# A dilated 3x3 convolution on one core: every load of x and every store cut into slices of 16 partitions

## The chip, the cores and the metric

The kernel runs on one core of a Trainium2 chip. The metric is the device time of one execution in microseconds. Each kernel was run several times; runs over 1.5% above the fastest of the same kernel are called slow, and the ratios below use fast runs alone. The program uses no other core of the chip.

## The reference

A convolution of 16 images (64 channels in, 128 out, 64x64 pixels, 3x3 taps, dilation 2, padding 2), all in float32.

```python
batch, c_in, h, w, c_out, k, dilation = 16, 64, 64, 64, 128, 3, 2
x_pad = np.pad(x, ((0, 0), (0, 0), (pad, pad), (pad, pad)), mode='constant')     # pad = 2
for kh in range(k):
    for kw in range(k):
        output[b, co] += weight[co, ci, kh, kw] * x_pad[b, ci, kh*dilation:kh*dilation+h, kw*dilation:kw*dilation+w]
```

x is 16.8 MB and the output 33.6 MB. With the weights the core must move about 50.6 MB.

## The kernel before

Two images at a time fill the 128 partitions (2 x 64 channels). One channel of one image is one DRAM row of 64 x 64 float32, 16 KB, and fills one SBUF partition. ACT casts x to float16, DVE adds row pairs, PE multiplies (it computes pairs of output rows with fewer products than the plain sum), ACT and DVE evacuate PSUM into a float32 output tile, and SP issues all loads and stores.

The parts that the change touches:

```python
x32pool = ctx.enter_context(tc.tile_pool(name="x32pool", bufs=3))
opool = ctx.enter_context(tc.tile_pool(name="opool", bufs=3))
# ... cut ...
def load(pb, rows):
    t = x32pool.tile([P, HW], f32, tag="x32", name="x32")
    x32_tiles[pb] = t
    lo = 0
    for hi in rows:
        nc.sync.dma_start(out=t[:, lo * W : hi * W], in_=x_pair[pb, :, lo * W : hi * W])
        lo = hi
# ... cut ...
def store(pb, m, lo, hi):
    nc.sync.dma_start(
        out=out_img[2 * pb + m, :, lo * W : hi * W],
        in_=o_tiles[pb][:, m * HW + lo * W : m * HW + hi * W],
    )
# ... cut ...
first = [[hi for _, hi in chunk_rows], [32 + d, H], [H]]   # pair 0 in four loads, pair 1 in two
for pb in range(min(3, npairs)):
    load(pb, first[pb])
# ... cut: the main loop over 32 groups of 16 image rows; at the end of a group ...
    if ahead[0] >= NG * (freed[0] + 1) and freed[0] + 3 < npairs:
        load(freed[0] + 3, [H])
        freed[0] += 1
    if pb == 0 and g % 2 == 1:
        for m in range(2):
            store(pb, m, (g - 1) * GR, (g + 1) * GR)
    elif pb > 0 and g == NG - 1:
        for m in range(2):
            store(pb, m, 0, H)
```

## Time and profile before

| what | value | where it is read |
|---|---|---|
| time | 129.94 us, median of 3 runs | runs |
| span of the profiled run | 126.5 us | page |
| PE busy | 83% | page, part 1 |
| DMA queue | 50.63 MB, 96.3% of 16 engines' span | page, part 3 |
| 16384-byte packets | 611 ns, at the 10th, 50th and 90th percentile | DMA packet records of the trace, 60 to 110 us |

These are lines of the page of the kernel before: the span in 40 equal slices (the busy share of the 16 DMA engines in tenths, and what they moved), then the queue, then two kinds of DMA issues (how many, the size of each, the median time from issue to landing).

```profile
DMA  4999999999999999999999999999999999989990
GB/s 134 319 410 405 456 420 409 386 425 427 438 443 404 300 420 414 432 425 445 425 414 435 427 435 425 425 430 425 435 425 430 435 425 430 425 383 425 425 430 26
q1 hardware_dynamic: 4464, 50.63, 96.3%
...
out_dram<-osb SPq DMA_DIRECT2D x14, 2048.0 KB, 15.6
```

The DMA engines are busy nearly everywhere at about 425 GB/s. The next line is a stretch of time from the windows view: start and end, length, busy us (and instructions) of PE, PE weight loads, DVE, ACT and POOL, then the granted clock, the DMA share and GB/s.

```profile
60.00:110.00 50.00, 50.00 (x488) 23.65 (x486) 42.94 (x47) 28.88 (x30) 0.00 (x0) 1.00 1.01 429
```

PE is busy throughout as well, but the timeline shows which of the two ends last: the last evacuation is over at 112.7 us, the last two stores are issued then, and the span ends at 126.5 us with transfers alone.

```profile
111.52 1.22 DVE L220 TENSOR_TENSOR osb<-psB,p_sb 128x1024 f32<-128x1024 f32 x1
112.76 0.81 SPq L100 DMA_DIRECT2D out_dram<-osb  x2
```

So the 50.63 MB set the time: at 429 GB/s they take 118 us of the 126.5. A packet of 16384 bytes in 611 ns is 26.8 GB/s, and 16 engines at that rate are 429 GB/s. That fits the Trainium skill, "DMA: Bandwidth & Descriptors", section "The descriptor swizzle": in a transfer of 128 partitions each engine writes one SBUF port of its own.

### The profile page before, as it was taken

The numbers are of one execution on the slowest core, as the hardware profiler recorded it, in microseconds if no ns is written. First come the engines' busy times: TensorE is split into PE (matmuls) and PEld (weight loads), VectorE is DVE, ScalarE is ACT, GpSimd is POOL, SyncE is SP. The second block draws the span as 40 slices with busy tenths as digits, with TensorE's granted clock in tenths as the row PEclk, the third lists the DMA queues.
The fourth block names the chain that finished last, engine by engine and source line by source line (L and its number), as shares of the span: only waits on it lengthen the run. The fifth ranks groups of instructions, "written<-read, shape, count | busy, mean of one in ns | idle before, by whom it ended". The sixth has DMA issues, their size and how long they took to land.

```text
span 126.5 us, 2316 instructions
## 1 busy us (share of the span) xinstructions
PE 105.4 (83%) x989; PEld 48.7 (39%) x989; DVE 89.9 (71%) x105; ACT 66.8 (53%) x71; POOL 0.7 (1%) x6
## 2 busy tenths in 40 slices
PE   6955988889999999999999999999999999920000
PEld 2522433334444444444444454445444444400000
DVE  0745667877889888988898888888888987760000
ACT  4767554746966666666667666666666433300000
POOL 2000000000000000000000000000000000000000
PEclk9999999999999999999999999999999999999555
DMA  4999999999999999999999999999999999989990
GB/s 134 319 410 405 456 420 409 386 425 427 438 443 404 300 420 414 432 425 445 425 414 435 427 435 425 425 430 425 435 425 430 435 425 430 425 383 425 425 430 26
DMA packets 4473, 50.76 MB, mean 401 GB/s; under 512 B 496, under 2 KB 496, under 8 KB 1264
## 3 DMA queue, kind: packets, MB, share of 16 engines
q1 hardware_dynamic: 4464, 50.63, 96.3%
q8 instruction: 7, 0.11, 0.3%
q14 instruction: 2, 0.02, 0.0%
HBM read 17.07 MB, written 33.55 MB: 400 GB/s over the span
## 4 chain that ended last, share of the span: by engine, by line
PE 67%; DVE 2%; DVEq 1%; ACT 1%; issue 0%
PE psA L164 27%; PE psB L164 25%; PE psP L164 14%; DVE osb L220 2%; DVEq L270 1%; ACT x_270 L87 1%; DVE xs L97 0%; DVEq L220 0%
## 5 line engine op out<-in xcount | busy, mean ns | idle before, releaser
L164 PEld LDWEIGHTS <-w_sb 64*128 64x128 f16 x960 | 46.2, 94 | 58.4 <-DVE xs L97 5.6
L216 ACT COPY p_sb<-psP 128x1024 f32<-128x1024 f32 x32 | 32.4, 1012 | 39.6 <-issue 23.4
L220 DVE TENSOR_TENSOR osb<-psA,p_sb 128x1024 f32<-128x1024 f32 x32 | 39.2, 1225 | 18.5 <-PE psA L164 14.8
L220 DVE TENSOR_TENSOR osb<-psB,p_sb 128x1024 f32<-128x1024 f32 x32 | 39.0, 1218 | 0.0
L164 PE MATMUL psP<-xs,w_sb 64*128 64x496 f16 (+1 forms) x192 | 25.6, 372 | 4.8 <-DVE xs L97 2.7
L164 PE MATMUL psB<-x_396,w_sb 64*128 64x496 f16 (+3 forms) x48 | 5.6, 365 | 0.0
L164 PE MATMUL psB<-x_848,w_sb 64*128 64x496 f16 (+3 forms) x48 | 5.6, 365 | 0.0
L164 PE MATMUL psA<-x_121,w_sb 64*128 64x496 f16 (+3 forms) x48 | 5.6, 365 | 0.0
L164 PE MATMUL psB<-x_522,w_sb 64*128 64x496 f16 (+3 forms) x48 | 5.6, 365 | 0.0
L164 PE MATMUL psB<-x_685,w_sb 64*128 64x496 f16 (+3 forms) x48 | 5.6, 365 | 0.0
L164 PE MATMUL psB<-x_121,w_sb 64*128 64x496 f16 (+3 forms) x48 | 5.6, 365 | 0.0
L164 PE MATMUL psA<-x_270,w_sb 64*128 64x496 f16 (+3 forms) x48 | 5.6, 365 | 0.0
L164 PE MATMUL psB<-x_270,w_sb 64*128 64x496 f16 (+3 forms) x48 | 5.6, 365 | 0.0
L164 PE MATMUL psB<-x_1009,w_sb 64*128 64x496 f16 (+3 forms) x48 | 5.6, 365 | 0.0
L164 PE MATMUL psB<-x_1170,w_sb 64*128 64x496 f16 (+3 forms) x48 | 5.6, 365 | 0.0
L164 PE MATMUL psA<-x_396,w_sb 64*128 64x496 f16 (+3 forms) x48 | 5.6, 365 | 0.0
L164 PE MATMUL psA<-x_848,w_sb 64*128 64x496 f16 (+3 forms) x48 | 5.6, 365 | 0.0
L164 PE MATMUL psA<-x_1009,w_sb 64*128 64x496 f16 (+3 forms) x48 | 5.6, 365 | 0.0
L164 PE MATMUL psA<-x_1170,w_sb 64*128 64x496 f16 (+3 forms) x48 | 5.6, 365 | 0.0
L164 PE MATMUL psA<-x_522,w_sb 64*128 64x496 f16 (+3 forms) x48 | 5.6, 365 | 0.0
L164 PE MATMUL psA<-x_685,w_sb 64*128 64x496 f16 (+3 forms) x48 | 5.6, 365 | 0.0
L122 PE MATMUL wp<-warm 128*128 128x512 f16 x14 | 4.5, 493 | 1.2 <-DVE warm L119 1.2
(34 smaller groups left out, 59.2 us busy)
## 6 DMA issues: line engine op xcount, KB each, us to landing
out_dram<-osb SPq DMA_DIRECT2D x14, 2048.0 KB, 15.6
out_dram<-osb SPq DMA_DIRECT2D x4, 1024.0 KB, 10.8
x_88<-in_x_dram SPq DMA_DIRECT2D x1, 2048.0 KB, 16.2
x_229<-in_x_dram SPq DMA_DIRECT2D x1, 2048.0 KB, 10.5
x_357<-in_x_dram SPq DMA_DIRECT2D x1, 2048.0 KB, 14.3
x_480<-in_x_dram SPq DMA_DIRECT2D x1, 2048.0 KB, 10.9
x_643<-in_x_dram SPq DMA_DIRECT2D x1, 2048.0 KB, 13.0
x_806<-in_x_dram SPq DMA_DIRECT2D x1, 2048.0 KB, 15.2
```

The costliest lines, as they stand in the source:

```text
L87: nc.scalar.copy(out=x16_tiles[pb][:, lo * W : hi * W], in_=x32_tiles[pb][:, lo * W : hi * W])
L122: nc.tensor.matmul(out=wp[:, 0:512], lhsT=warm[:, 0:P], rhs=warm)
L164: nc.tensor.matmul(out=po, lhsT=w_sb[pp, t * CO : (t + 1) * CO], rhs=rhs, start=first and j == 1, stop=last and j == 2,)
L216: nc.scalar.copy(out=p_sb, in_=psP)
L220: nc.vector.tensor_tensor(out=o[:, :, b0 : b0 + NBLK, e], in0=ps.rearrange("p (m b q) -> p m b q", m=2, q=2 * W), in1=pv, op=add,)
L270: with _tile.TileContext(nc) as tc:
```

## The change

The intent, as its author put it: every transfer in slices of 16 partitions, so that neighbouring DRAM rows go to different DMA rings. Before, one engine takes eight rows of a transfer; after, each of 16 engines takes one row of each slice.

```diff
+    PD = 16
@@ load
         for hi in rows:
-            nc.sync.dma_start(out=t[:, lo * W : hi * W], in_=x_pair[pb, :, lo * W : hi * W])
+            for p in range(0, P, PD):
+                nc.sync.dma_start(
+                    out=t[p : p + PD, lo * W : hi * W],
+                    in_=x_pair[pb, p : p + PD, lo * W : hi * W],
+                )
             lo = hi
@@ store
-        nc.sync.dma_start(
-            out=out_img[2 * pb + m, :, lo * W : hi * W],
-            in_=o_tiles[pb][:, m * HW + lo * W : m * HW + hi * W],
-        )
+        for p in range(0, P, PD):
+            nc.sync.dma_start(
+                out=out_img[2 * pb + m, p : p + PD, lo * W : hi * W],
+                in_=o_tiles[pb][p : p + PD, m * HW + lo * W : m * HW + hi * W],
+            )
```

The built program has 241 DMAs instead of 31. It has eight completion semaphores for them, used in turn, so every slice also waits until the slice eight before it has landed.

## The prediction

> **What bounds the kernel now.** The DMA engines. The page's slice line shows DMA at 9 tenths in nearly every slice, 400 GB/s mean, and about 425 GB/s from slice 5 to the end. The queue line gives q1 96.3% of 16 engines' span. 50.63 MB at 425 GB/s is 119 us of a 126.5 us span. The median 16384-byte packet takes 611 ns, 26.8 GB/s for each of 16 engines, 429 GB/s together. TensorE (PE 83%) fills the chain of waits, but the last evacuation ends near 112.7 us (timeline), and 13 us of stores follow. So compute has slack; transfer time does not. A perfect 429 GB/s throughout would win some 3% at best.
>
> **What the change does.** The instructions of PE, DVE, ACT and POOL keep their order. Only the SP queue changes: 31 transfers become 241 (all but the weight load cut in eight). Bytes and row lengths stay, so packet counts stay about 4464. Three effects:
>
> 1. Issue. One x load's issue took 0.34 us when idle (timeline), 0.5 us during the start. If a slice costs the same 0.34 us, 241 issues are 82 us of SP, mostly hidden: a 256 KB slice needs 0.6 us at 429 GB/s. Not hidden at the start: the first six loads' 48 slices cost about 16 us of issue against 3 us before. I estimate 3 to 6 us lost.
>
> 2. Waits. The order listing shows each slice waiting for the slice eight before it. Eight 256 KB slices are 2 MB in flight, 4.9 us of work, enough; eight 64 KB slices are 512 KB, 1.2 us of work, less than one landing (2.9 us for the weights). This also slows the start.
>
> 3. Ports, the main term. The Trainium skill, "SBUF — State Buffer", section "Door 1: The DMA port swizzle", says 16 neighbouring partitions reach 4 of 16 SBUF ports, measured there at 104 GB/s (asymptote 109). Before, all 128 partitions were in each transfer and every engine had its own port. After, engine i takes one row of each slice, so four engines meet on one port and all 16 engines walk through the slices together. In full lock-step that is 50.63 MB / 109 GB/s, about 465 us. With eight slices queued, engines that get ahead move to other ports, so I expect partial overlap: about 300 GB/s, 169 us plus 6 us of start and end. No trace here shows a port conflict yet; that is the uncertain step.
>
> **Critical path.** All of effect 3 lies on it, since DMA bounds every stage.
>
> **Predicted:** 175 us; eight in ten between 132 and 320. Faster 0.04, same 0.09, slower 0.87.
>
> **What the profile would show.** Port conflict: the 16384-byte packets take well over 611 ns, GB/s in the slices falls to 150 to 350 while DMA busy stays high, PE share falls, and the chain of waits is filled by store and load landings (osb and x32 buffers). Only issue cost: packets stay at 611 ns, DMA busy falls, SP is nearly solid with issues of 0.3 us or more. Neither: slices at 425 GB/s from about slice 6 on and a time near 131 to 136 us.
>
> **What would make it wrong.** Engines spreading over the ports so well that 425 GB/s is kept: then about 132 us. Full lock-step: 400 us or more. An issue costing 0.6 us or more: SP becomes the limit. Neighbouring rows on different engines helping DRAM: gains at most 3%.

## The result, and the profile after

The changed kernel takes 277.63 us (median of 4 runs, 276.36 to 280.94) against 129.85 us (4 runs). Its fast runs are 2.136 times as long, 95% interval 2.122 to 2.150. Ratios here are the mean time of one kernel's fast runs over that of the other's of the same rounds, so not quite the ratio of the quoted medians. The result is correct.

The same lines of the page, after:

```profile
DMA  5469999998989999989999999998999989889895
GB/s 148 142 142 128 134 115 124 124 119 106 258 198 227 127 138 129 138 313 210 201 150 301 241 212 189 337 227 189 215 212 204 208 186 203 203 181 205 189 205 119
q1 hardware_dynamic: 7824, 50.64, 92.3%
...
out_dram<-osb SPq DMA_DIRECT2D x112, 256.0 KB, 5.1
```

The bytes are the same (50.64 MB) and the engines are as busy as before (92.3%), but they move less than half as much per microsecond. The packet count grows by 3360, which is 210 more DMAs times 16: each DMA has 16 packets of 4 bytes besides its data. The data packets are the same in number and size.

Three stretches by the windows view, with the columns as before:

```profile
40.00:65.00 25.00, 15.22 (x134) 7.21 (x131) 11.04 (x14) 7.25 (x8) 0.00 (x0) 0.80 0.99 115
95.00:115.00 20.00, 8.66 (x70) 4.28 (x71) 7.20 (x9) 6.91 (x8) 0.00 (x0) 0.64 1.01 131
225.00:265.00 40.00, 0.00 (x0) 0.00 (x0) 0.00 (x0) 0.00 (x0) 0.00 (x0) 0.51 0.92 199
```

By the issue times and the landings, only loads are moved in the first two, and only stores in the third, with no compute at all any more. The page's median hides that these are two different regimes. The packet records of the trace, counted by their start, tell them apart:

| 16384-byte packets of the changed kernel | 10th percentile, ns | median, ns | 90th, ns |
|---|---|---|---|
| 40 to 65 us (loads) | 2202 | 2205 | 2222 |
| 95 to 115 us (loads) | 1993 | 1994 | 1995 |
| 225 to 265 us (stores) | 611 | 1178 | 1869 |
| whole run (before: 611 ns) | | 1307 | |

While loads run, nearly all rows of a stretch take the same time, 3.3 to 3.6 times as long as before, and the packets start in groups of 16. I call this *in step*. Stores are spread from the undisturbed 611 ns to three times that.

SP now spends nearly the whole run issuing, or waiting to issue (start and length, merged, with the number of DMAs; the first x loads and stores, and the last stores):

```profile
1.18 14.78 SPq L80 DMA_DIRECT2D x_80<-in_x_dram  x32
16.01 11.70 SPq L80 DMA_DIRECT2D x_113<-in_x_dram  x16
28.32 7.00 SPq L80 DMA_DIRECT2D x_130<-in_x_dram  x8
37.27 15.85 SPq L80 DMA_DIRECT2D x_278<-in_x_dram  x8
56.32 28.86 SPq L106 DMA_DIRECT2D out_dram<-osb  x32
...
165.49 104.43 SPq L106 DMA_DIRECT2D out_dram<-osb  x80
```

In the kernel before, the first store was issued at 17.5 us. Here it is at 56.3 us. The waits view of SP tells waiting from issuing (what SP waited for, us in total, times, longest us):

```profile
SPq L80 <- DMA x_130<-in_x_dram: 15.1, 8, 1.9
SPq L106 <- DMA x_939<-in_x_dram: 7.0, 7, 1.1
SPq L106 <- DMA out_dram<-osb: 0.4, 2, 0.3
```

In a stage of loads SP waits about 1.9 us for the slice eight before, issues in 0.31 us, and has seven other slices in flight. In the last 80 stores it hardly waits: 7.0 us for the last loads, 0.4 us for stores. There the issues themselves fill the time, 1.2 us each, against 0.42 us at the start of the run. One store is issued every 1.3 us and lands 5.1 us later (page), so about four are under way, not eight. Whether the long issue holds the transfers up, or slow transfers hold the issue up, this trace can't say.

### The profile page after: what moved, and what is told of

Read it like the earlier page. It is cut to its first block, busy times and chain, and to the rows that moved or that the text cites. A ratio compares the mean times of both kernels' runs of the same rounds, so it can differ in the third digit from the quotient of the medians.

```text
span 274.6 us, 2590 instructions
## 1 busy us (share of the span) xinstructions
PE 123.2 (45%) x989; PEld 57.7 (21%) x989; DVE 89.6 (33%) x105; ACT 66.8 (24%) x71; POOL 0.7 (0%) x6
## 3 DMA queue, kind: packets, MB, share of 16 engines
q1 hardware_dynamic: 7824, 50.64, 92.3%
## 4 chain that ended last, share of the span: by engine, by line
DMA 26%; SPq 22%; PE 3%; DVE 2%; issue 2%; DVEq 0%
SPq L106 21%; DMA out_dram<-osb 15%; DMA x_571<-in_x_dram 6%; DMA x_755<-in_x_dram 2%; DMA x_441<-in_x_dram 2%; DVE osb L226 2%; DMA x_939<-in_x_dram 2%; PE psB L170 1%; PE psA L170 1%; PE psP L170 1%; SPq L80 0%; DVEq L276 0%; DVE xs L102 0%; DVEq L226 0%
## 5 line engine op out<-in xcount | busy, mean ns | idle before, releaser
L170 PEld LDWEIGHTS <-w_sb 64*128 64x128 f16 x960 | 54.8, 102 | 158.1 <-issue 104.1
L170 PE MATMUL psP<-xs,w_sb 64*128 64x496 f16 (+1 forms) x192 | 30.6, 428 | 43.5 <-ACT p_sb L222 30.7
L170 PE MATMUL psB<-x_818,w_sb 64*128 64x496 f16 (+3 forms) x48 | 6.9, 426 | 17.4 <-DVE osb L226 17.4
L170 PE MATMUL psB<-x_1002,w_sb 64*128 64x496 f16 (+3 forms) x48 | 6.9, 426 | 14.6 <-DVE osb L226 14.6
L170 PE MATMUL psB<-x_1177,w_sb 64*128 64x496 f16 (+3 forms) x48 | 6.9, 425 | 10.5 <-DVE osb L226 10.5
L170 PE MATMUL psB<-x_1352,w_sb 64*128 64x496 f16 (+3 forms) x48 | 6.9, 425 | 6.4 <-DVE osb L226 6.4
L92 ACT CAST x_818<-x_441 128x1024 f16<-128x1024 f32 (+2 forms) x4 | 4.2, 1047 | 22.2 <-DMA x_441<-in_x_dram 22.2
L170 PE MATMUL psB<-x_634,w_sb 64*128 64x496 f16 (+3 forms) x48 | 6.9, 425 | 4.3 <-DVE osb L226 4.3
L170 PE MATMUL psA<-x_340,w_sb 64*128 64x496 f16 (+3 forms) x48 | 7.6, 463 | 0.0
L92 ACT CAST x_487<-x_130 128x1024 f16<-128x1024 f32 (+2 forms) x4 | 4.1, 1046 | 12.3 <-DMA x_130<-in_x_dram 12.3
L92 ACT CAST x_340<-x_113 128x1024 f16<-128x1024 f32 (+2 forms) x4 | 4.2, 1046 | 11.4 <-DMA x_113<-in_x_dram 11.4
L128 PE MATMUL wp<-warm 128*128 128x512 f16 x14 | 6.0, 624 | 1.2 <-DVE warm L125 1.2
L170 PE MATMUL psA<-x_634,w_sb 64*128 64x496 f16 (+3 forms) x48 | 6.5, 410 | 0.0
L170 PE MATMUL psA<-x_1002,w_sb 64*128 64x496 f16 (+3 forms) x48 | 6.4, 405 | 0.0
L92 ACT CAST x_634<-x_278 128x1024 f16<-128x1024 f32 (+2 forms) x4 | 4.2, 1047 | 9.0 <-DMA out_dram<-osb 9.0
L170 PE MATMUL psA<-x_487,w_sb 64*128 64x496 f16 (+3 forms) x48 | 6.3, 400 | 0.0
L170 PE MATMUL psA<-x_1177,w_sb 64*128 64x496 f16 (+3 forms) x48 | 5.6, 365 | 0.0
L170 PE MATMUL psA<-x_1352,w_sb 64*128 64x496 f16 (+3 forms) x48 | 5.6, 365 | 0.0
L170 PE MATMUL psA<-x_818,w_sb 64*128 64x496 f16 (+3 forms) x48 | 5.6, 365 | 0.0
```

The source lines that it names most:

```text
L92: nc.scalar.copy(out=x16_tiles[pb][:, lo * W : hi * W], in_=x32_tiles[pb][:, lo * W : hi * W])
L128: nc.tensor.matmul(out=wp[:, 0:512], lhsT=warm[:, 0:P], rhs=warm)
L170: nc.tensor.matmul(out=po, lhsT=w_sb[pp, t * CO : (t + 1) * CO], rhs=rhs, start=first and j == 1, stop=last and j == 2,)
```

## The experiments

Theories:

- **Port theory.** 16 neighbouring partitions lie on 4 SBUF ports. The Trainium skill, "SBUF — State Buffer", section "Door 1: The DMA port swizzle (why `[64,N]` ≈ `[32,N]`)", gives the port of a partition: bits 4 to 2 and bit 6 of its number choose it. Four engines then share one port.
- **Count theory.** 241 DMAs cost too much: SP's issue time, and the wait for the DMA eight before.
- **DRAM theory.** 16 neighbouring DRAM rows read or written at one time collide in DRAM.

16 kernels ran. "Per port" is the number of engines that meet on a port while all work on the same slice, by the skill's map and with neighbouring rows of a slice on one engine (the packet records don't name the engine); "order" is how the port sets of successive slices follow each other, a letter for each set.

The median is over all runs, fast and slow; the ratio is of the fast ones.

| run | slice | per port | order | DMAs | median us | ratio to before (95%) |
|---|---|---|---|---|---|---|
| before | 128 partitions | 1 | A | 31 | 129.85 | 1 |
| the change | 16 neighbours | 4 | ABABCDCD | 241 | 277.63 | 2.136 (2.122 to 2.150) |
| e1 | 16, step 8 | 2 | AAAABBBB | 241 | 226.49 | 1.748 (1.735 to 1.761) |
| e2 | 16, step 8 in SBUF only | 2 | AAAABBBB | 241 | 227.21 | 1.755 (1.740 to 1.769) |
| e3 | 16, step 8 in DRAM only | 4 | ABABCDCD | 241 | 271.38 | 2.099 (2.077 to 2.121) |
| e4 | 128, 1/8 of the columns | 1 | A | 241 | 160.84 | 1.240 (1.227 to 1.253) |
| e5 | 32 neighbours | 2 | AABB | 121 | 182.89 | none, see there |
| e6 | 64 neighbours | 2 | AB | 61 | 161.70 | 1.251 (1.225 to 1.277) |
| e7 | 16, loads only | 4 | ABABCDCD | 115 | 205.27 | 1.576 (1.551 to 1.601) |
| e8 | 16, stores only | 4 | ABABCDCD | 157 | 205.21 | 1.588 (1.570 to 1.605) |
| e9 | 16, reordered | 4 | ABCDABCD | 241 | 275.27 | 2.122 (2.104 to 2.140) |
| e10 | as e4, first 6 loads whole | 1 | A | 199 | 145.17 | 1.120 (1.111 to 1.128) |
| e11 | as e8, 2 images per DMA | 4 | ABABCDCD | 85 | 197.81 | 1.501 (1.484 to 1.519) |
| e12 | 128, stores in halves | 1 | A | 45 | 128.86 | 0.994 (0.988 to 0.999) |
| e13 | as e1, reordered | 2 | ABABABAB | 241 | 199.07 | 1.534 (1.518 to 1.550) |
| e14 | 64, 1/4 of the columns | 2 | ABABABAB | 241 | 204.86 | 1.583 (1.569 to 1.598) |
| e15 | 32, step 4 | 2, one row later on the other 8 ports | A | 121 | 137.19 | 1.060 (1.049 to 1.071) |
| e16 | as e14, grouped | 2 | AAAABBBB | 241 | 228.78 | 1.765 (1.753 to 1.778) |

The results of e2 and e3 are wrong on purpose (rows land in other partitions, relative error 1.41 in both). All others are correct.

### Which side: e1, e2, e3

A step of 8 between the partitions of a slice, with everything else as in the changed kernel.

```diff
-                    out=t[p : p + PD, lo * W : hi * W],
-                    in_=x_pair[pb, p : p + PD, lo * W : hi * W],
+                    out=t[p // PD :: P // PD, lo * W : hi * W],            # e1, e2
+                    in_=x_pair[pb, p // PD :: P // PD, lo * W : hi * W],   # e1, e3
```

The stores were edited in the same way.

> Slices of 16 rows with a step of 8 (rows s, s+8, ..., s+120) instead of 16 neighbours, on both sides, so the result is right. Same 241 DMAs, same bytes per DMA, same waits as the changed kernel. By the skill's port map these 16 partitions lie on 8 ports, two engines on each. Port theory: about half the sharing, 150 to 200 us, median 16384-byte packet well under the 1307 ns of the changed kernel. DRAM theory (16 neighbouring DRAM rows read at once collide): about 130 to 140 us. Count theory (eight times as many DMAs, each waiting for the one eight before): unchanged, about 278 us.

> Step of 8 on the SBUF side only; the DRAM side keeps 16 neighbouring rows. The result is wrong on purpose (rows land in other partitions). Port theory: equal to the run with the step on both sides within 5%. DRAM theory: as the changed kernel, about 278 us. Count theory: 278 us.

> Step of 8 on the DRAM side only; the SBUF side keeps 16 neighbouring partitions. The result is wrong on purpose. Port theory: as the changed kernel, 265 to 290 us. DRAM theory: equal to the run with the step on both sides, far below 278. Count theory: 278 us.

Measured: 226.49, 227.21 and 271.38 us. The step in SBUF alone does as much as the step on both sides. The step in DRAM alone leaves the time within 3% of the changed kernel. These are a stretch of loads and one of stores of e1, then the same of e2:

```profile
35.00:45.00 10.00, 7.79 (x74) 3.32 (x69) 5.71 (x7) 3.38 (x5) 0.00 (x0) 1.00 1.00 211
180.00:215.00 35.00, 1.22 (x14) 0.47 (x10) 2.35 (x2) 0.00 (x0) 0.00 (x0) 0.58 0.94 235
```

```profile
35.00:45.00 10.00, 8.14 (x78) 3.52 (x73) 5.71 (x7) 3.71 (x5) 0.00 (x0) 1.00 1.02 218
180.00:215.00 35.00, 2.47 (x26) 1.17 (x22) 3.08 (x3) 1.01 (x1) 0.00 (x0) 0.61 0.94 237
```

The median load packet of the first stretch is 1249 ns in e1 and 1246 ns in e2, against 2205 ns in the changed kernel (40 to 65 us). Two engines per port: 2.0 times 611 ns; four: 3.3 to 3.6 times. In e3 the loads stay at 2098 ns (40 to 65 us). So the DRAM theory falls as the main cause, and the place of the conflict is the SBUF side, with sizes near those that the port map asks for (2 and 4). My expectation of 150 to 200 us for e1 was too low. The DMA count is the same in all these runs, so it can't make the difference between them, but it may be part of all of them.

### The count alone: e4 and e10

Eight slices again, but along the columns, each with all 128 partitions: the same 241 DMAs, bytes per DMA and waits, and no shared port.

```diff
-            for p in range(0, P, PD):
-                nc.sync.dma_start(
-                    out=t[p : p + PD, lo * W : hi * W],
-                    in_=x_pair[pb, p : p + PD, lo * W : hi * W],
-                )
+            n = (hi - lo) * W // 8                # e10: // (8 if pb > 1 else 1)
+            for q in range(lo * W, hi * W, n):
+                nc.sync.dma_start(out=t[:, q : q + n], in_=x_pair[pb, :, q : q + n])
```

The stores are cut the same way in both.

> Each transfer again cut in eight, but along the columns: every slice has all 128 partitions and an eighth of each row (2 KB of a 16 KB row). Same 241 DMAs, same bytes per DMA, same wait for the DMA eight before. Port theory: close to the kernel before, 130 to 142 us, the excess being the slower start (issue of 48 slices). Count theory: about 278 us as the changed kernel.

> The column slices (all 128 partitions, an eighth of each row) again, but the six loads of the first two pairs whole. If the 31 us that the column slices cost came from the start, where eight 56 to 136 KB slices in flight don't cover one landing, this is 132 to 142 us. If they came from 2 KB rows or from issue all along, 150 us or more.

Measured: 160.84 us for e4 and 145.17 us for e10. Both expectations of the port theory were too low, though the count theory in its pure form (278 us) falls. The page of e4:

```profile
DMA  4645488899874879999999999999999999999995
GB/s 129 160 139 131 99 255 263 240 399 386 295 256 151 267 177 328 326 399 406 405 317 362 405 402 376 348 397 399 406 402 402 379 389 387 385 387 386 384 380 222
```

In the first 20 us the engines are half idle (5 to 20 us: DMA share 0.51, 128 GB/s). SP's own time is what holds them there:

```profile
1.17 34.72 SPq L81 DMA_DIRECT2D x<-in_x_dram  x64
```

The first 32 of these slices are issued one every 0.47 us (median), 64 KB in the mean, which is 138 GB/s. The waits view of the first 25 us shows no wait for a DMA: the slice eight before had always landed. With the first six loads whole, which saves 42 of these issues, 16 us of the 31 us come back. The other 15 us I didn't take apart: 2 KB rows (380 to 389 GB/s at the end instead of 429), the issue time and the wait for DMAs of 128 and 256 KB are all candidates. So the count, with the rows that this form of it shortens, costs 31 us, against the 148 us of the change. It doesn't reproduce the 1.2 us that SP takes for a late store of the change: the late stores of e4 take 0.6 us each.

### The slice size: e5 and e6

```diff
-    PD = 16
+    PD = 32        # e5; e6: PD = 64
```

> Slices of 32 neighbouring partitions: four DMAs where the changed kernel has eight, 121 in all. By the skill's port map 32 neighbours lie on 8 ports, two engines on each, like the run with the step of 8. Port theory: packets as there (1.2 to 1.3 us where engines are in step), 200 to 226 us, the gain over 226 being the cheaper start. Count theory: half of the way or more back to 130, about 160 us or less.

> Slices of 64 neighbouring partitions, two per transfer, 61 DMAs in all. By the skill's port map 64 neighbours still lie on only 8 ports. Port theory: as with 32 partitions within 10%, 190 to 225 us, with packets near 1.2 us. Count theory: 132 to 140 us, since the DMAs are only doubled and each is 1 MB.

e5 took 182.20, 183.58 and 185.54 us in three runs, all called slow against a fourth of 174.32 us, so there is no interval and I draw no number from it: 174 to 186 us. e6 took 161.70 us. That misses the port theory's 190 to 225 us and also the count theory's 132 to 140. The windows view of e6 shows why it fits neither, first a stretch of loads, then a later one:

```profile
25.00:35.00 10.00, 9.54 (x90) 4.20 (x87) 6.66 (x8) 4.92 (x6) 0.00 (x0) 1.00 1.02 218
90.00:125.00 35.00, 31.34 (x278) 15.79 (x276) 24.26 (x28) 17.73 (x19) 0.00 (x0) 0.90 1.00 419
```

The loads begin in step, as in e1 (median packet 1253 ns). Later nine packets in ten take 634 ns or less, although every slice still lies on 8 ports only. That fits engines that share a port having moved to different slices, on different ports, so that sharing a port costs only engines that meet there at the same time. The packet records don't name the engine, so this is a reading, to be tested below.

### Loads and stores apart: e7 and e8

e7 keeps the slices for loads and has whole stores; e8 has the reverse.

```diff
-        for p in range(0, P, PD):                 # e7: in store(); e8: the same in load()
-            nc.sync.dma_start(
-                out=out_img[2 * pb + m, p : p + PD, lo * W : hi * W],
-                in_=o_tiles[pb][p : p + PD, m * HW + lo * W : m * HW + hi * W],
-            )
+        nc.sync.dma_start(
+            out=out_img[2 * pb + m, :, lo * W : hi * W],
+            in_=o_tiles[pb][:, m * HW + lo * W : m * HW + hi * W],
+        )
```

> Loads in slices of 16 partitions, stores whole as before. In the changed kernel load packets ran in step at 2.0 to 2.2 us, about 125 GB/s: 16.8 MB of x take 134 us there against 39 us at 429 GB/s. Port theory: if transfer times add up, 130 + 95 = about 225 us at most, less where waiting engines go on to stores. Count theory: 96 loads of 200 extra DMAs, mostly the start, about 150 us.

> Stores in slices of 16 partitions, loads whole as before. Store packets in the changed kernel had about 200 GB/s where only stores ran: 33.6 MB take 168 us against 78 us at 429 GB/s. Port theory: 130 + 90 = about 220 us at most. Count theory: the start is whole again, 130 to 140 us.

Measured: 205.27 and 205.21 us in the median. By the ratios of the fast runs the sliced loads cost 0.576 and the sliced stores 0.588 of the kernel before, together 1.164, about 151 us; the whole change costs 1.136, 148 us. The two halves add up. Stretches of loads and of whole stores in e7, then of sliced stores in e8:

```profile
40.00:65.00 25.00, 16.73 (x124) 7.43 (x122) 11.05 (x14) 7.73 (x8) 0.00 (x0) 0.73 1.01 118
160.00:195.00 35.00, 21.63 (x192) 10.79 (x191) 20.57 (x21) 8.04 (x9) 0.00 (x0) 0.84 1.00 428
```

```profile
150.00:195.00 45.00, 2.99 (x30) 1.45 (x26) 3.59 (x4) 1.01 (x1) 0.00 (x0) 0.59 0.92 199
```

Each kind of slice has about the rate that it has in the changed kernel (118 against 115 GB/s, 199 in both), and whole stores are back at 428. In e8 the start is whole, and the cost is still 0.588 of the kernel before, some 76 us: the stores' share isn't the start.

### How far apart engines may run: e9, e11, e13, e14, e16

e6 suggested a refinement, which I then tried. Engines on one port run freely once they are some slices apart. The wait for the slice eight before, less the slices that pass during one landing, limits how far apart they can be. In e9 the order of slices makes the needed distance shorter; in e11 each slice lasts longer.

```diff
-            for p in range(0, P, PD):
+            for p in (0, 16, 64, 80, 32, 48, 96, 112):     # e9, loads and stores
```

```diff
+        if m == 1:                                          # e11, in store(); loads are whole
+            return
         for p in range(0, P, PD):
             nc.sync.dma_start(
-                out=out_img[2 * pb + m, p : p + PD, lo * W : hi * W],
-                in_=o_tiles[pb][p : p + PD, m * HW + lo * W : m * HW + hi * W],
+                out=out[2 * pb : 2 * pb + 2, p : p + PD].rearrange("m p h w -> p m (h w)")[
+                    :, :, lo * W : hi * W],
+                in_=o_tiles[pb][p : p + PD].rearrange("p (m q) -> p m q", m=2)[
+                    :, :, lo * W : hi * W],
             )
```

> The changed kernel with its eight slices in another order: partitions 0, 16, 64, 80, 32, 48, 96, 112. Same DMAs, same count, result right. The four port sets then come round as ABCD ABCD instead of AB AB CD CD. Four engines that share ports run free of each other when they are 0, 1, 2 and 3 slices apart; in the changed kernel they must be up to 5 apart, and each slice waits for the one eight before to land. Port theory with this limit: stores well above 200 GB/s, in all 200 to 250 us; load packets that are in step may stay at 2.0 to 2.2 us, which keeps it above 200. Count theory or a fixed port average: 270 to 285 us, as the changed kernel.

> Loads whole, stores in slices of 16 partitions as in the run with sliced stores alone (205 us), but each DMA carries both images of a pair: two rows per engine, 512 KB, so eight in flight are 4 MB. Same port map, same order. If the limit on how far engines run apart (eight slices less one landing of 2 us or more) holds the stores at 200 GB/s, a slice that takes twice as long leaves more slices of spread: 145 to 190 us. If port sharing alone sets 200 GB/s whatever is queued: 200 to 210 us.

e9 took 275.27 us: no change, and its stores (202 GB/s from 225 to 265 us) are no faster. e11 took 193.93 and 195.39 us in its two fast runs (ratio 1.501 against 1.588 for e8), 5% less than e8 and still above the range that I gave. For four engines to a port, the forecasts of the refinement failed. So I tried it with two engines to a port, varying the order of the port sets (e13 against e1, e14 against e16) and the bytes in flight (e14 against e6).

```diff
-            for p in range(0, P, PD):                       # e13: on top of e1
+            for s in (0, 4, 1, 5, 2, 6, 3, 7):              #   rows s :: 8
```

```diff
+            n = (hi - lo) * W // 4                          # e14; e16 has the two loops swapped
+            for q in range(lo * W, hi * W, n):
+                for p in range(0, P, 64):
+                    nc.sync.dma_start(
+                        out=t[p : p + 64, q : q + n], in_=x_pair[pb, p : p + 64, q : q + n]
+                    )
```

> The run with the step of 8 (226 us, two engines on a port), with its eight slices in the order 0, 4, 1, 5, 2, 6, 3, 7. By the port map the two port sets then alternate (ABABABAB) instead of coming four and four (AAAABBBB): two engines that share a port are free of each other when they are one slice apart, instead of four. If how far apart engines may run sets the rate: stores near 400 GB/s, 150 to 185 us. If not: 220 to 230 us.

> Slices of 64 partitions and a quarter of the columns: 256 KB each and 241 DMAs, as in the changed kernel, port sets alternating as in the run with 64-partition slices, which reached 410 to 430 GB/s with up to 8 MB in flight. Now at most 2 MB are in flight. If the depth of the queue let the engines spread there, stores fall to about 230 GB/s: 210 us or more. If alternating ports are enough: stores near 380 GB/s after the first loads, 170 to 185 us with the slow start of small DMAs.

> As the run with 64 partitions and quarter columns, but all four quarters of one half of the partitions first, then of the other: port sets come AAAABBBB. Same DMAs, bytes and window. If the offset that engines need counts: slower than with alternating sets, about 215 to 230 us. If not: equal to it.

Here the order counts. Grouped sets give 226.49 us (e1) and 228.78 us (e16), alternating sets 199.07 us (e13) and 204.86 us (e14). The two ways to cut (16 partitions with a step of 8, or 64 neighbours and a quarter of the columns) agree within 3% in each order, though their DRAM patterns, SBUF patterns and row lengths differ; what they share is the port map, the order, the 241 DMAs and the 2 MB in flight. Late stretches of e13, e14 and e16:

```profile
150.00:190.00 40.00, 11.66 (x112) 6.17 (x108) 10.37 (x10) 3.88 (x4) 0.00 (x0) 0.68 0.82 277
```

```profile
150.00:190.00 40.00, 14.67 (x144) 7.47 (x140) 13.07 (x13) 5.90 (x6) 0.00 (x0) 0.72 0.84 275
```

```profile
180.00:215.00 35.00, 3.35 (x34) 1.56 (x30) 3.95 (x4) 1.01 (x1) 0.00 (x0) 0.61 0.92 237
```

e14 has the port order of e6, with DMAs of 256 KB instead of 1 MB and so at most 2 MB in flight instead of 8. It stays at 275 GB/s where e6 has 419. Its shorter rows (4 KB) are not the reason: with rows of 2 KB and own ports, e10 had 393 GB/s from 90 to 130 us. Note the DMA share of 0.82 to 0.84 in e13 and e14 too: engines there also stand idle, waiting for the next DMA. With two engines to a port, then, the order counts, and so does the size of the DMAs. Whether by the bytes in flight or by SP's issue isn't shown: from 150 to 190 us of e14 SP issues almost without a pause, 0.89 us each, and one DMA of 256 KB every 0.94 us is 278 GB/s. Alternating sets didn't reach the 400 GB/s that I expected, so the refinement has the direction right and not the size.

The traces show one premise of the refinement to be wrong: in the late stores it isn't the wait for the slice eight before that limits how far apart engines can be. In the changed kernel, e8 and e9 that slice had landed some 5 us before the next issue (median), and three others were in flight. The changed kernel also shows stores with more in flight. Three times, about when the last load of a stage lands, seven other slices, by then all or nearly all stores, are queued. The first three lines of this windows view show those moments, the fourth what follows the last of them:

```profile
121.00:124.00 3.00, 0.00 (x0) 0.00 (x0) 0.00 (x0) 2.64 (x3) 0.00 (x0) 0.84 1.05 371
149.00:152.00 3.00, 1.81 (x18) 0.81 (x15) 0.00 (x0) 2.68 (x3) 0.00 (x0) 1.00 1.03 399
174.00:178.00 4.00, 4.00 (x44) 2.26 (x42) 2.92 (x4) 2.84 (x4) 0.00 (x0) 1.00 1.03 414
180.00:200.00 20.00, 9.49 (x74) 4.47 (x72) 8.47 (x10) 5.14 (x6) 0.00 (x0) 0.74 0.89 203
```

So slices of 16 neighbours, four engines to a port, were stored at 371 to 414 GB/s (median packet 611 ns) while the queue was full. Then SP took about 1 us and more for each issue, the queue ran down to about four, and the rate fell to about 200. That fits engines being free of each other once they are apart; e9 didn't keep its queue any fuller (three others in flight). No run changed the issue time alone, so whether the long issue is the cause of the 200 GB/s or its result stays open.

### Small slices on all ports: e15

Slices of 32 partitions with a step of 4: one DMA covers all 16 ports. Compare with e5, which has the same 121 DMAs of the same sizes on 8 ports.

```diff
-    PD = 16
+    PD = 32
-                    out=t[p : p + PD, lo * W : hi * W],
-                    in_=x_pair[pb, p : p + PD, lo * W : hi * W],
+                    out=t[p // PD :: P // PD, lo * W : hi * W],
+                    in_=x_pair[pb, p // PD :: P // PD, lo * W : hi * W],
```

> Slices of 32 partitions with a step of 4 (121 DMAs, 512 KB), so that one DMA covers all 16 ports and each engine takes two rows on two neighbouring ports; compare with 32 neighbours (174 to 186 us). If each engine takes two consecutive rows of the slice, the first rows lie on 8 ports and the second on the other 8: in step still 1.27 us per packet, but one row of offset frees them, 135 to 165 us. If a different split, packets of 611 ns from the start and about 135 us. If offset does not matter: 174 to 186 us as with 32 neighbours.

Measured: 137.19 us, against 174 to 186 us for e5. Of the page of e15:

```profile
DMA  4776899999998999999999999999999999999950
GB/s 129 220 215 188 300 348 390 436 392 426 416 409 322 436 329 404 419 431 419 436 421 436 421 426 426 426 426 426 436 416 436 416 440 426 421 431 421 441 228 15
```

After the start it runs at the rate of the kernel before (median packet 611 ns over the whole run). Some early packets take 900 ns and more, as if engines met at first and then parted. The 7 us that remain against the kernel before lie in the start (at 15 MB moved, e15 is 7 us behind), where the slices are 112 to 144 KB, SP issues one every 0.64 us and the DMA share is 0.6 to 0.8. This is the plainest pair: the same number of DMAs and bytes, neighbours against every fourth partition, and some 40 us between them. (The step is on the DRAM side too; by e1 and e2 that side makes no difference.)

### A cut that costs nothing: e12

```diff
-        if pb == 0 and g % 2 == 1:
+        if g % 2 == 1:
             for m in range(2):
                 store(pb, m, (g - 1) * GR, (g + 1) * GR)
-        elif pb > 0 and g == NG - 1:
-            for m in range(2):
-                store(pb, m, 0, H)
```

> The kernel before, with every store cut in two along the image rows as soon as half an image is done (all 128 partitions, 1 MB), as it already does for the first pair. No port sharing. It may fill the one dip of the DMA line (300 GB/s in the slice at 41 to 44 us): 127.5 to 131 us, so within 2%. Count theory: 14 DMAs more, under 1 us worse.

128.86 us (6 runs, 128.57 to 129.10) against 130.14 us (9 runs): ratio 0.994, interval 0.988 to 0.999. That is the same at 2%, and just over half a per cent faster. The page of e12 no longer has the dip to 300 GB/s that the page of before shows in its fourteenth slice:

```profile
GB/s 125 313 405 431 450 413 397 382 433 428 436 436 400 444 436 400 426 428 436 415 408 423 439 428 408 426 418 418 433 423 421 428 421 426 431 423 433 423 294 28
```

It is the only kernel that beats both, by very little, since by my estimate only some 3% was there to win.

## Why the prediction was wrong

The direction, the bound and the mechanism were right; the size was not. I forecast 175 us, 45 more than before; it became 277.63, 148 more. That lies within my range, 132 to 320, but at more than three times the forecast change.

- *DMA bounds the kernel.* Right: bytes unchanged, busy share unchanged, and the time follows the rate (185 GB/s on the page of after, against 401).
- *Port conflict as the main term.* Right, and shown by e2 against e3 and by e15 against e5. The failed step is the term "partial overlap: about 300 GB/s, 169 us". It measured 115 to 131 GB/s in two stretches of loads and 199 GB/s in the long stretch of stores, 185 GB/s over the run. "With eight slices queued, engines that get ahead move to other ports" failed in two ways. Loads had eight slices queued and stayed in step all the same: nearly all packets took 2.2 or 2.0 us. Stores did spread, at up to 414 GB/s while the queue was full, but it didn't stay full: some four were under way, and the rate was about 200. Sliced stores alone and sliced loads alone cost about 76 us each.
- *Full lock-step would be 465 us* (my estimate, from the skill's 109 GB/s). The rate in step was a little better (115 to 131), and only the loads, a third of the bytes, ran so.
- *Issue: 0.34 us for each slice, mostly hidden; start: 3 to 6 us lost.* Too small. A slice at the start took 0.42 us, a late store 1.2 us. "An issue costing 0.6 us or more: SP becomes the limit" stood among the things that would make me wrong, and SP was indeed busy issuing throughout the late stores. The first 48 slices took SP 26.5 us, some 4 of them waiting, where I had put 16. What the start cost in the changed kernel was not isolated: e10 gave back 16 us of e4's 31 by taking the first six loads whole, with slices of another form. There the issue was the limit, not the 512 KB in flight.
- *Profile signs.* Packets well over 611 ns (1307 in the median) with high busy (92.3%): right. Slices at 150 to 350 GB/s: the slices with loads alone lay lower, at 106 to 148. A packet count of about 4464: wrong, it became 7824, with the 4-byte packets of the added DMAs. "The chain of waits is filled by store and load landings": right in part; it names DMA 26% and the SP queue 22%, and PE 3% instead of 67%.
- *Neighbouring rows on different engines help DRAM.* No sign of it: e3, which undoes that part, takes 271 us.

What stays open: why loads stay in step with seven others in flight and stores don't; why SP takes 1.2 us to issue a late store, and whether that is what holds the stores at about 200 GB/s with four engines to a port; what the start costs in the changed kernel; and the split of e10's last 15 us. Waits alone were not taken away, since the eight semaphores belong to the program's framework.

## What to carry to other kernels

Before cutting a transfer by partitions, work out which SBUF ports each slice covers: a slice of neighbours puts several engines on one port, and if they start together they can stay together. Cut along the free axis (halves cost nothing in e12, eighths 15 to 31 us in e10 and e4), or take every fourth partition (7 us in e15), so that each DMA reaches all ports. And look at what the issuing queue does before blaming a wait: at the start of e4 SP issued a DMA of 64 KB every 0.47 us without waiting, and that alone held the transfers at about 138 GB/s.

## What the Trainium skill lacked or had wrong

- "SBUF — State Buffer", "Door 1: The DMA port swizzle": no run contradicts its map of partitions to ports. Its rate for 16 neighbours, 104 GB/s at 1 MiB (asymptote 109), is a little low for a stream of slices: 115 to 131 GB/s in step, with packets 3.3 to 3.6 times the undisturbed 611 ns, not 4 times. It doesn't say that stores of such slices, out of step, get more: 199 GB/s with about four in flight, 371 to 414 with a full queue.
- "SBUF — State Buffer", "Can I just issue two DMAs to hit both halves?": it answers no, the only way to all 16 ports being one transfer over all 128 partitions. With slices of 64 partitions and 1 MB each in the queue, e6 ran at 419 GB/s from 90 to 125 us. And 32 partitions with a step of 4, which span the 128 without filling them, are enough: e15, 428 GB/s from 80 to 125 us (windows view).
- No page tells that engines sharing a port may stay in step for tens of microseconds, or that the order of the slices changes the rate (e1 226.49 us, e13 199.07 us, with the same DMAs).
- No page tells that SP's issue of a store can take longer when little else is in flight: 1.2 us for 256 KB late in the changed kernel, against 0.31 us for the stores that were issued while loads ran in step.
